# A feed-forward block's opening: one plain chunk in place of two, and two product pairs whose gate blocks are also loaded plain

## Chip, cores and metric
The kernel runs on one core of one Trainium2 chip. The metric is device time in microseconds (us) of one execution. The kernel before takes 2849.59 us (median of three runs, 2848.89 to 2852.01).

## What is computed
A two-layer encoder trunk in fp32 over 768 tokens (512 of one request, 256 of another), model width 1024. Each layer is feed-forward, token mixer, feed-forward:

```python
def swiglu_ffn(x, w1, w2):            # w1: 1024 x 5632, w2: 2816 x 1024
    gate, up = jnp.split(x @ w1, 2, axis=-1)
    return (jax.nn.silu(gate) * up) @ w2

for li in range(2):
    x = x + 0.5 * swiglu_ffn(rmsnorm(x, norm_g[li, 0]), ffn_w1[li, 0], ffn_w2[li, 0])
    x = x + mixer(rmsnorm(x, norm_g[li, 1]))     # layer 0 HGRN2, layer 1 windowed attention
    x = x + 0.5 * swiglu_ffn(rmsnorm(x, norm_g[li, 2]), ffn_w1[li, 1], ffn_w2[li, 1])
```

The change touches only the four feed-forward blocks, called f0 to f3 here in the order in which they run (f0, HGRN2, f1, f2, window attention, f3).

## The kernel before
**Numbers.** Every fp32 factor is split into a rounded part hi and a remainder lo, and a product is three matmuls: hi by hi, hi by lo, lo by hi. ScalarE (ACT) makes hi by a cast, VectorE (DVE) makes lo by a subtraction; for weights these are L166 with L167 (1024 wide) or L199 with L200, for activations both stand in `split` (L266, L267).

**Chunks and products.** The hidden width of 2816 is 22 chunks of 128. A chunk has a gate block and an up block of the weights, each 1024 by 128. Tokens are taken in two halves of 384, the model width in two halves of 512. A chunk is computed in one of two ways:

- *Plain* (`up_plain`): for each token half, 24 matmuls of 128x384 for gate and 24 for up, 96 for the chunk (L261 to L263).
- *Pair* (`up_pair`): gate and up, with the two token halves, make a 2x2 block product that is done by Strassen's seven products (Winograd's form), p1 to p7, of 12 matmuls each, 84 in all (L421). The weight side is combined from four quarter blocks a11, a12 (gate) and a21, a22 (up), the token side from b00, b10, b01, b11 (model half, token half) and four sums t1 to t4. p1 and p2 use b00 and b10 only, and p1 + p2 is just the gate block of the first token half. p7 uses t3, p5 t1, p4 t4, p6 t2, and p3 uses b11.

**Order of a feed-forward block.** `ffn` goes through five groups g of four chunks: up products of the group, then `down_quad`, 126 matmuls of 128x512 (L479), whose results are added to x by DVE (L501). Two chunks are left for the end. In group 0 of every block the first two chunks are plain, and they go first: chunk 0 and chunk 1 on token half 0, then both on token half 1; only then come the pairs of chunks 2 and 3. The reason for plain work in front is in the code's deferred steps: when a block begins, only the first token half has been normalised and transposed. `run_later`, called in the plain chunks' loops, carries out one deferred step at a time between matmuls: the transposes of the second half in two parts (`turn`, L323 and L326, with splits L266 and L267), and `sums`, which makes t1 to t4 by eight subtractions of 128x768 on DVE (L350, L351, L353, L354) and eight splits of 128x768 (ACT L266, DVE L267).

**Weights.** A queue (`plan`, `plan_quad`) lists every weight block in the order of use. `load_next` brings raw blocks into a ring of four raw tiles `wr` (512 KB each, on SP's DMA queue); a pair takes two of them, one for gate and one for up, and for p7 a third small tile `s` (256 KB). GpSimd's queue (POOL) issues accumulating DMAs (`into`, L141): s += a11, and a21 += a22 in place. The remaining combinations are DVE additions in place: a11 += a21 (L206, behind the split for p1) and a12 += a11 (L210, behind the split for p2); they are called the **first add** and the **second add** below. Each split fills a tile of a ring `w` of eight; `held` counts them, and `done` frees one and stages the next steps of the queue as far as eight allow. So a raw tile is free once the last split that reads it has run, and the next load of the queue goes into it. A `down_quad` takes four raw tiles at once, and its first add is 1024 wide.

**Order on the engines.** The program is written in the order of these calls, and a scheduler arranges the instructions of each engine; each engine then carries its own list out strictly in order, waiting on semaphores.

Of the kernel before, what the change touches and what calls it, by code (L numbers as in the profile page):

```python
# [12 lines left out]
AF = mybir.ActivationFunctionType  # L13
# [23 lines left out]
PLAIN = 2  # L37
# [5 lines left out]
UP = ("p1", "p7", "p2", "p5", "p4", "p6", "p3")  # L43
DOWN = ("p1", "p2", "p5", "p4", "p7", "p6", "p3")
# [3 lines left out]
class Trunk:  # L48
# [123 lines left out]
    def quad_steps(self, key, raws, srcs, order):  # L172
# [31 lines left out]
        def p1():  # L204
            split("p1", [a11])
            nc.vector.tensor_add(a11, a11, a21)  # L206

        def p2():
            split("p2", [a12])
            nc.vector.tensor_add(a12, a12, a11)  # L210

        steps = {
            "p1": p1,
            "p2": p2,
            "p3": lambda: split("p3", [a12]),
            "p4": lambda: split("p4", [a22]),
            "p5": lambda: split("p5", [a21], nc.gpsimd if up else None),
            "p6": lambda: split("p6", [a11]),
            "p7": lambda: split("p7", s3),
        }  # L220
        return [(1 if up else 2, steps[name]) for name in order]
# [176 lines left out]
    def up_plain(self, tag, j, half):  # L398
        pss = []
        for c in range(2):  # L400
            wh, wl = self.take((tag, j, c))
            ps = self.ps(H)
            for k in range(NC):
                b = self.operand(f"b{k // 4}{half}", k % 4)
                self.mm3(ps, (wh[:, k, :], wl[:, k, :]), b, k == 0, k == NC - 1)
                if half == 0 and k in (((), (2, 6)), ((3, 7), (3, 7)))[j][c]:
# [9 lines left out]
    def product(self, key, name, src, ps, first, last):  # L416
        wh, wl = self.take((*key, name))
        for k in range(4):
            a, b = (wh[:, k, :], wl[:, k, :]), self.operand(src, k)
# [9 lines left out]
        self.done((*key, name))  # L429

    def up_pair(self, tag, j):
        nc = self.nc
        key = (tag, j)
        a, b, c, d = (self.ps(H) for _ in range(4))
        v, w, t = (self.tmp(H) for _ in range(3))
        p = lambda name, ps, first, last: self.product(key, name, FACTOR[name], ps, first, last)
        p("p1", a, True, False)
        nc.scalar.copy(v, a)
        p("p7", c, True, False)
        nc.scalar.copy(w, c)  # L440
        p("p2", a, False, True)
        nc.scalar.activation(a, a, AF.Silu)
# [60 lines left out]
    def ffn(self, tag, next_row):  # L503
        for g in range(GROUPS):
# [7 lines left out]
            def gather(ts, kp):  # L512
                self.mix(ts[0], ts[1], ts[2], ts[3], lambda name, src: put(name, src, kp))

            if g == 0:
                ts = {}
                for half in range(2):
                    for j in range(PLAIN):
                        t = ts[2 * j + half] = self.up_plain(tag, j, half)
                        name = f"b{j}{half}"  # L520
                        if name != "b01":
                            put(name, t, 0)
                gather(ts, 0)
                self.run_later(len(self.deferred))
            for kp in range(2):
                if g == 0 and kp == 0:
                    continue
                ts = []
                for j in range(2):
                    for half, t in enumerate(self.up_pair(tag, 4 * g + 2 * kp + j)):  # L530
# [751 lines left out]
```

## Time and profile before
| | |
|---|---|
| median of three runs | 2849.59 us |
| profiled execution | 2852.12 us |
| its span | 2850.3 us (1.8 us lie around it) |
| mean granted TensorE clock | 0.998 |
| busy: PE, DVE, ACT, POOL | 98%, 76%, 46%, 12% |
| L421 (pair products) | 6720 matmuls of 128x384 |
| L479 (down products) | 2520 matmuls of 128x512 |

Starts of the stages of group 0, in us from the span's start:

| block | first pair product | first down product |
|---|---|---|
| f0 | 55.31 | 85.17 |
| f1 | 1106.00 | 1135.12 |
| f2 | 1605.54 | 1634.66 |
| f3 | 2382.71 | 2411.83 |

In a timeline row the columns are start, duration, engine, line, operation, output and inputs, form, and count; a bracket at the end gives the idle time ahead and what ended it. Matmuls overlap, so their cost is the distance of their starts and not their duration: the 84 of one pair take 14.57 us (0.1735 each), 18 of a down product 4.28 (about 0.23 each with what follows). The same holds for DVE, whose duration of 0.95 for a 128x768 subtraction goes with starts 0.87 apart, and in the same way 0.60 for 512 wide, 0.47 for 384 wide and 1.13 for 1024 wide.

### The profile page before, as it was taken

Reading aid. Unit: us, or ns where it says so; the run is one execution under the profiler, and the core shown is the slowest. Engines: PE = TensorE matmul, PEld = TensorE weight load, DVE = VectorE, ACT = ScalarE, POOL = GpSimd, SP = SyncE. Lnnn points to the kernel's source line nnn. Section 1 sums busy time; section 2 is a strip of 40 time slices with the busy share of each in tenths; the row PEclk is TensorE's granted clock in tenths of the full one; section 3 lists DMA queues with packets and bytes.
Section 4 is the critical chain, followed back from the end, with each engine's and each line's share of the span. In section 5 each row is a group of like instructions: output and inputs, shape, how many; then the busy total and the mean of one; then the engine's idle time right before and its main releaser. Section 6 shows DMA issues by size and latency. Waiting matters only on the chain. (4 is left out here: it accounts for less than half of the span.)

```text
span 2850.3 us, 40558 instructions
## 1 busy us (share of the span) xinstructions
PE 2796.7 (98%) x15225; PEld 2554.2 (90%) x15225; DVE 2173.2 (76%) x3750; ACT 1318.9 (46%) x2454; POOL 355.1 (12%) x402
## 2 busy tenths in 40 slices
PE   8999999999999999999999999999999899999998
PEld 8899999889899889998998998999888789989997
DVE  7788787468577658878878887887848878788877
ACT  7344443434344336434444643444458755434443
POOL 1111111000000001111111111111002211111110
PEclk9999999999999999999999999999999999999999
DMA  6554454311111133555444355545422113555443
GB/s 165 127 125 122 116 134 121 115 44 39 44 39 38 60 97 86 132 127 122 123 119 114 84 134 127 122 121 124 126 71 75 37 51 90 135 126 125 117 121 96
DMA packets 330101, 291.37 MB, mean 102 GB/s; under 512 B 11608, under 2 KB 257840, under 8 KB 329904
## 3 DMA queue, kind: packets, MB, share of 16 engines
q1 hardware_dynamic: 294064, 212.43, 25.4%
q0 software_dynamic: 31680, 62.93, 12.6%
q10 hardware_dynamic: 4160, 13.42, 1.3%
q8 instruction: 119, 1.95, 0.3%
q14 instruction: 78, 0.64, 0.1%
HBM read 216.39 MB, written 9.44 MB: 79 GB/s over the span
## 5 line engine op out<-in xcount | busy, mean ns | idle before, releaser
L421 PE MATMUL ps<-big,w 128*128 128x384 f32 x6720 | 1172.8, 334 | 3.1 <-DVE tA L444 2.9
L421 PEld LDWEIGHTS ps<-big,w 128*128 128x128 f32 x6720 | 1165.4, 188 | 8.8 <-DVE tA L444 7.2
L199 ACT CAST w<-wr 128x512 fp32r<-128x512 f32 x600 | 416.1, 707 | 722.7 <-PE ps L421 321.0
L479 PE MATMUL ps<-w,big 128*128 128x512 f32 x2520 | 586.8, 391 | 17.4 <-DVE x L501 17.4
L479 PEld LDWEIGHTS ps<-w,big 128*128 128x128 f32 x2520 | 469.4, 188 | 129.7 <-DVE x L501 17.3
L200 DVE TENSOR_TENSOR w<-wr,w 128x512 fp32r<-128x512 f32 (+1 forms) x520 | 438.1, 853 | 95.7 <-ACT w L199 87.0
L501 DVE SCALAR_TENSOR_TENSOR x<-ps,x 128x512 f32<-128x512 f32 x468 | 305.5, 682 | 20.5 <-PE ps L479 10.2
L141 POOL DMA_DIRECT2D s<-wr x120 | 105.4, 878 | 1333.4 <-DMA wr<-in_ffn_w_dram 583.0
L261 PE MATMUL ps<-w,big 128*128 128x512 f32 x624 | 249.8, 400 | 0.2
L263 PE MATMUL ps<-w,big 128*128 128x512 f32 x624 | 245.2, 393 | 2.5 <-DVE big L330 1.3
L262 PE MATMUL ps<-w,big 128*128 128x512 f32 x624 | 244.4, 392 | 0.0
L266 ACT CAST big<-tA 128x384 fp32r<-128x384 f32 x296 | 148.0, 513 | 175.0 <-DVE tA L449 72.0
L261 PE MATMUL ps<-big,w 128*128 128x384 f32 (+2 forms) x640 | 220.8, 346 | 3.3 <-ACT big L266 2.0
L262 PE MATMUL ps<-big,w 128*128 128x384 f32 (+2 forms) x640 | 216.8, 339 | 0.7 <-DVE big L267 0.5
L263 PE MATMUL ps<-big,w 128*128 128x384 f32 (+2 forms) x640 | 215.7, 337 | 0.0
L167 DVE TENSOR_TENSOR w<-wr,w 128x1024 fp32r<-128x1024 f32 x92 | 111.6, 1222 | 83.6 <-ACT w L166 59.7
L141 POOL DMA_DIRECT2D wr<-wr x100 | 87.5, 875 | 680.0 <-DVE tA L350 319.8
L267 DVE TENSOR_TENSOR big<-tA,big 128x384 fp32r<-128x384 f32 x296 | 164.2, 566 | 7.9 <-ACT big L266 4.4
L206 DVE TENSOR_TENSOR wr<-wr,wr 128x512 f32<-128x512 f32 (+1 forms) x100 | 79.3, 793 | 114.5 <-DMA wr<-wr 85.9
L166 ACT CAST w<-wr 128x1024 fp32r<-128x1024 f32 x92 | 96.6, 1052 | 120.5 <-PE ps L262 99.7
L263 PEld LDWEIGHTS ps<-w,big 128*128 128x128 f32 x624 | 117.4, 188 | 28.8 <-DVE big L330 2.0
L261 PEld LDWEIGHTS ps<-w,big 128*128 128x128 f32 x624 | 117.8, 189 | 22.3 <-issue 0.6
(170 smaller groups left out, 3317.2 us busy)
## 6 DMA issues: line engine op xcount, KB each, us to landing
wr<-in_ffn_w_dram SPq DMA_DIRECT2D x264, 512.0 KB, 3.9
s<-in_ffn_w_dram SPq DMA_DIRECT2D x120, 256.0 KB, 3.0
s<-wr POOLq DMA_DIRECT2D x120, 256.0 KB, 4.0
wr<-wr POOLq DMA_DIRECT2D x80, 256.0 KB, 4.0
wr<-in_hg_w_in_dram SPq DMA_DIRECT2D x40, 512.0 KB, 3.8
wr<-wr POOLq DMA_DIRECT2D x20, 512.0 KB, 4.6
spill<-x ACTq DMA_DIRECT2D x12, 512.0 KB, 3.0
x<-spill ACTq DMA_DIRECT2D x12, 512.0 KB, 3.3
```

Source lines behind the costliest of these rows:

```text
L141: self.nc.gpsimd.dma_start(out, src, accum_op=ALU.add)
L167: self.nc.vector.tensor_sub(lo, raw, hi.bitcast(F32))
L199: nc.scalar.copy(h, src)
L200: (eng or nc.vector).tensor_sub(l, src, h.bitcast(F32))
L261: nc.tensor.matmul(out, a[0], b[0], start=first, stop=False)
L262: nc.tensor.matmul(out, a[0], b[1], start=False, stop=False)
L263: nc.tensor.matmul(out, a[1], b[0], start=False, stop=last)
L266: self.nc.scalar.copy(hi, src)
L267: self.nc.vector.tensor_sub(lo, src, hi.bitcast(F32))
L421: self.nc.tensor.matmul(ps, a[x], b[y], start=first and k == 0 and i == 0, stop=k == 3 and i == 2, skip_group_check=True,)
L479: nc.tensor.matmul(ps, a[x], w[y], start=name == chain and kp == 0 and q == 0, stop=kp == 1 and q == 2, skip_group_check=True,)
L501: self.nc.vector.scalar_tensor_tensor(x, ps, c, x, ALU.mult, ALU.add)
```

## The change
Only chunk 0 stays plain. Chunks 1 and 2 become pairs that are *opened*: their gate blocks are loaded and split a second time as plain 1024-wide tiles (key "gate"), and between the two token halves of chunk 0 `open_pairs` multiplies these by b00 (p1 of both) and b10 (p2 of both). That gives the gate of the first token half, and with it p1's value for the rest. After the second token half of chunk 0, the opened pairs compute only p7, p5, p4, p6 and p3 (the order `REST`). In that order the first add stands behind the split for p7 and the second behind that for p4, and the lo split of p5 runs on DVE, where an unopened pair has it on GpSimd. Chunk 3 is a whole pair as before. Deferred steps run at k = 2 and 6 of chunk 0's up block and after each of the four products of `open_pairs`.

```diff
-PLAIN = 2
+PLAIN = 1
+OPENED = range(PLAIN, PLAIN + 2)
+REST = ("p7", "p5", "p4", "p6", "p3")
...
+        own = {"p1": [a11], "p2": [a12], "p3": [a12], "p4": [a22], "p5": [a21], "p6": [a11], "p7": s3}
+        second = lambda: nc.vector.tensor_add(a11, a11, a21)
+        fourth = lambda: nc.vector.tensor_add(a12, a12, a11)
+        after = {"p7": second, "p4": fourth} if order == REST else {"p1": second, "p2": fourth}
+        def step(name):
+            split(name, own[name], nc.gpsimd if order == UP and name == "p5" else None)
+            if name in after:
+                after[name]()
...
             if i < PLAIN:
                 self.plan((tag, i, 0), gate, (NC, P))
                 self.plan((tag, i, 1), up, (NC, P))
+                for j in OPENED:
+                    self.plan((tag, j, "gate"), w1[:, j * P : (j + 1) * P], (NC, P))
             else:
-                self.plan_quad((tag, i), (gate, up), (NC, P), UP)
+                self.plan_quad((tag, i), (gate, up), (NC, P), REST if i in OPENED else UP)
...
+    def open_pairs(self, tag, js):
+        opened = {j: (self.ps(H), self.tmp(H)) for j in js}
+        for part in range(2):
+            for j, (a, v) in opened.items():
+                key = (tag, j, "gate")
+                w = tuple(t[:, 4 * part : 4 * part + 4, :] for t in self.take(key))
+                self.multiply(a, w, FACTOR["p2" if part else "p1"], not part)
+                if part:
+                    self.done(key)
+                    self.nc.scalar.activation(a, a, AF.Silu)
+                else:
+                    self.nc.scalar.copy(v, a)
+                self.run_later()
+        return opened
...
             if g == 0:
-                for half in range(2):
-                    for j in range(PLAIN):
-                        t = ts[2 * j + half] = self.up_plain(tag, j, half)
...
+                plain = [self.up_plain(tag, 0, 0)]
+                put("b00", plain[0], 0)
+                opened = self.open_pairs(tag, OPENED)
                 self.run_later(len(self.deferred))
+                plain.append(self.up_plain(tag, 0, 1))
```

In the changed file the lines move: the first add is L207, the second L208, the weight splits L169 and L202, the activation splits L261 and L262, the subtractions of `sums` L345, L346, L348 and L349, the plain matmuls L256 to L258, the down matmuls L496; the pair products stay L421.

Per feed-forward block the instruction lists differ so: 96 plain matmuls less, 84 pair matmuls more (24 of them in `open_pairs`), so 12 matmuls less; two loads of 512 KB more, one of 256 KB more, two accumulating DMAs more; on DVE one pair's worth of combinations (seven instructions of 128x384) and four weight splits of 512 more, one first and one second add more, two multiplications less; on GpSimd one split less.

Three places show how the lists move; names are the program's own tiles.

**f0, DVE, the weights of the second chunk.** Before: wr_186 and wr_188 are the raw gate and up blocks of chunk 1, x_108 is the last block of tokens, big_274 the transposed second half.

```order
L306 TENSOR_SCALAR big_252<-x_108,stat_253 128x1024
L167 TENSOR_TENSOR w_307<-wr_186,w_306 128x1024
L167 TENSOR_TENSOR w_395<-wr_188,w_394 128x1024
L464 TENSOR_TENSOR x_108<-x_108 128x512
L267 TENSOR_TENSOR big_291<-big_274,big_291 128x2x384
L267 TENSOR_TENSOR big_294<-big_274,big_294 128x2x384
```

After: wr_186 and wr_188 are the plain gate blocks of chunks 1 and 2, wr_194 and wr_196 the raw blocks of the pair of chunk 1.

```order
L301 TENSOR_SCALAR big_252<-x_108,stat_253 128x1024
L207 TENSOR_TENSOR wr_194<-wr_194,wr_196 128x512
L169 TENSOR_TENSOR w_311<-wr_186,w_310 128x1024
L208 TENSOR_TENSOR wr_194<-wr_194 128x512
L481 TENSOR_TENSOR x_108<-x_108 128x512
L262 TENSOR_TENSOR big_291<-big_274,big_291 128x2x384
L262 TENSOR_TENSOR big_294<-big_274,big_294 128x2x384
L262 TENSOR_TENSOR big_303<-tA_300,big_303 128x384
L262 TENSOR_TENSOR big_348<-big_331,big_348 128x2x384
L262 TENSOR_TENSOR big_351<-big_331,big_351 128x2x384
L169 TENSOR_TENSOR w_355<-wr_188,w_354 128x1024
```

Both adds of the pair of chunk 1 now stand around the split of the first gate block, and the split of the second gate block (on ACT its cast too) stands behind the splits of the second token half.

**f1, DVE, the start of `sums`.** big_9086 and big_9125 (before), big_9101 and big_9140 (after) are the transposed second half. Before:

```order
L267 TENSOR_TENSOR big_9103<-big_9086,big_9103 128x2x384
L267 TENSOR_TENSOR big_9106<-big_9086,big_9106 128x2x384
L267 TENSOR_TENSOR big_9142<-big_9125,big_9142 128x2x384
L267 TENSOR_TENSOR big_9145<-big_9125,big_9145 128x2x384
L350 TENSOR_TENSOR big_9125<-big_9086,big_9125 128x768
L413 TENSOR_TENSOR tA_9151<-tA_9151,ps_9072 128x384
L351 TENSOR_TENSOR big_9086<-big_8961,big_9086 128x768
```

After, with wr_9020 and wr_9022 the raw blocks of the pair of chunk 2:

```order
L262 TENSOR_TENSOR big_9118<-big_9101,big_9118 128x2x384
L262 TENSOR_TENSOR big_9121<-big_9101,big_9121 128x2x384
L207 TENSOR_TENSOR wr_9020<-wr_9020,wr_9022 128x512
L208 TENSOR_TENSOR wr_9020<-wr_9020 128x512
L262 TENSOR_TENSOR big_9157<-big_9140,big_9157 128x2x384
L262 TENSOR_TENSOR big_9160<-big_9140,big_9160 128x2x384
L345 TENSOR_TENSOR big_9140<-big_9101,big_9140 128x768
L410 TENSOR_TENSOR tA_9166<-tA_9166,ps_9087 128x384
L346 TENSOR_TENSOR big_9101<-big_8976,big_9101 128x768
```

The two adds of chunk 2's pair are now in front of the splits and of the whole chain of `sums`. On PE the first pair products there are, before, p1, p7 and p2 of chunk 2 (big_8978 and big_9041 are operands of the first token half, big_9180 and big_9196 the two model quarters of t3):

```order
L421 MATMUL ps_9397<-big_8978,w_9270 128x384 x6
L421 MATMUL ps_9397<-big_8981,w_9270 128x384 x6
L421 MATMUL ps_9399<-big_9180,w_9274 128x384 x6
L421 MATMUL ps_9399<-big_9196,w_9274 128x384 x6
L421 MATMUL ps_9397<-big_9041,w_9302 128x384 x6
L421 MATMUL ps_9397<-big_9044,w_9302 128x384 x6
```

and after, p7 of chunk 1 with pieces of p5 (big_9199 and big_9215 are the quarters of t3, big_9191 and big_9207 those of t1):

```order
L421 MATMUL ps_9350<-big_9199,w_9246 128x384 x6
L421 MATMUL ps_9351<-big_9191,w_9250 128x384 x3
L421 MATMUL ps_9350<-big_9215,w_9246 128x384
L421 MATMUL ps_9351<-big_9191,w_9250 128x384 x3
L421 MATMUL ps_9351<-big_9207,w_9250 128x384 x4
L421 MATMUL ps_9350<-big_9215,w_9246 128x384 x5
```

PE's first pair product no longer uses the first half's operands but t3.

**f1, DVE, the end of chunk 3's pair.** Before, wr_9005 and wr_9007 are its raw blocks; the splits of w_9481 and w_9496 are for p6 and p3:

```order
L200 TENSOR_TENSOR w_9465<-wr_9007,w_9465 128x512
L200 TENSOR_TENSOR w_9481<-wr_9005,w_9481 128x512
L447 TENSOR_TENSOR tA_9401<-tA_9401,ps_9398 128x384
L200 TENSOR_TENSOR w_9496<-wr_9005,w_9496 128x512
L448 TENSOR_TENSOR tA_9403<-ps_9399,tA_9401 128x384
```

After, wr_9302 and wr_9304 are its raw blocks, and w_9511 and w_9526 are for p6 and p3:

```order
L202 TENSOR_TENSOR w_9511<-wr_9302,w_9511 128x512
L346 TENSOR_TENSOR tA_9346<-tA_9166,tA_9346 128x384
L348 TENSOR_TENSOR tA_9166<-tA_9166,tA_9352 128x384
L464 TENSOR_TENSOR tA_9175<-tA_9175,ps_9462 128x384
L262 TENSOR_TENSOR big_9448<-tA_9346,big_9448 128x384
L349 TENSOR_TENSOR tA_9353<-tA_9353,tA_9166 128x384
L202 TENSOR_TENSOR w_9526<-wr_9302,w_9526 128x512
```

The hidden chunks' own sums (384 wide), which before ran ahead of these splits, now stand between the splits for p6 and p3 of chunk 3, the last that read its raw tiles.

More of the change, by code (lines that the diff above doesn't have):

```diff
@@ L202, in split @@
             self.staged[(*key, name)] = (view(hi), view(lo), 1 if up else 2)
[L204 to L221, printed above, removed]
+        own = {"p1": [a11], "p2": [a12], "p3": [a12], "p4": [a22], "p5": [a21], "p6": [a11], "p7": s3}
[6 more added lines that the diff above has]
+                after[name]()
+        return [(1 if up else 2, lambda name=name: step(name)) for name in order]
     def stage_next(self):
@@ L428, in product, with up_pair @@
                 )
-        self.done((*key, name))
-    def up_pair(self, tag, j):
+    def open_pairs(self, tag, js):
[12 more added lines that the diff above has]
+        return opened
+    def up_pair(self, tag, j, opened=None):
         nc = self.nc
         key = (tag, j)
[L434 to L438, printed above, removed]
+        a, v = opened or (self.ps(H), self.tmp(H))
+        b, c, d = (self.ps(H) for _ in range(3))
+        w, t = (self.tmp(H) for _ in range(2))
+        p = lambda name, ps, first, last: self.product(key, name, FACTOR[name], ps, first)
+        if not opened:
+            p("p1", a, True, False)
+            nc.scalar.copy(v, a)
         p("p7", c, True, False)
         nc.scalar.copy(w, c)
-        p("p2", a, False, True)
-        nc.scalar.activation(a, a, AF.Silu)
+        if not opened:
+            p("p2", a, False, True)
+            nc.scalar.activation(a, a, AF.Silu)
         p("p5", d, True, False)
```

24 lines of the change are left out of this document (12 added, 12 removed).

## The prediction
> **What bounds the kernel now.** I read the page first, then PE's waits, then the chain of waits, and then timelines at the head of each feed-forward block.
>
> ```profile
> span 2850.3 us, 40558 instructions
> PE 2796.7 (98%) x15225; PEld 2554.2 (90%) x15225; DVE 2173.2 (76%) x3750; ACT 1318.9 (46%) x2454; POOL 355.1 (12%) x402
> L421 PE MATMUL ps<-big,w 128*128 128x384 f32 x6720 | 1172.8, 334 | 3.1 <-DVE tA L444 2.9
> ```
> ```profile
> PE ps L479 <- DVE x L501: 17.4, 37, 0.5
> ```
> ```profile
> 2382.87 14.57 PE ps L421 x84
> ```
>
> TensorE is busy 98% of the span, so work taken from it counts in full as long as the other engines keep feeding it. A matmul of 128x384 costs 14.57/84 = 0.1735 us in a dense stream. PE's largest wait is for DVE in the down products, 37 times at most 0.5 us. So the kernel is bound by PE, with DVE second, and DVE's 76% is a mean over unequal stages:
>
> ```profile
> 1064.00:1106.00 42.00, 41.91 (x254) 40.64 (x252) 37.63 (x51) 31.64 (x56) 3.89 (x3) 1.00 0.20 46
> 1106.00:1135.00 29.00, 29.00 (x169) 29.00 (x169) 21.44 (x34) 14.37 (x25) 3.96 (x4) 1.00 0.46 118
> 1135.00:1165.00 30.00, 29.39 (x129) 23.69 (x128) 29.50 (x48) 10.11 (x18) 4.75 (x5) 1.00 0.56 138
> ```
>
> These are f1's plain stage, its two pairs and its first down products (length, then busy time of PE, weight loads, DVE, ACT, POOL). DVE works 37.6 of 42 us in the first and 29.5 of 30 in the third: beside the plain chunks and in the down products nothing can be added to it, or made late on it, without PE noticing. Only beside the pairs is there slack.
>
> **What goes.** The program's lists have 12 matmuls less per block: 12 x 0.1735 = 2.08 us, four times 8.3 us (0.29%). That is certain, since it is in the instruction lists; the rest is whether PE gets its operands in time.
>
> **Step 1: the t-sums are wanted earlier.** Chunk 0 on its second half takes 48 matmuls where two chunks took 96, so p7, the first product on t3, comes 48 x 0.1735 = 8.33 us before the old end of the plain stage. In f1:
>
> ```profile
> 1106.00 0.68 PE L421 MATMUL ps<-big,w 128*128 128x384 f32 x3
> ...
> 1135.12 4.28 PE L479 MATMUL ps<-w,big 128*128 128x512 f32 x18
> 1139.57 0.70 PE L479 MATMUL ps<-w,big 128*128 128x512 f32 x2 [0.17 <-DVE x L501]
> ```
> ```profile
> 1078.76 1.83 DVE L267 TENSOR_TENSOR big<-big,big 128x768 fp32r<-128x768 f32 x2 [1.52 <-ACT big L266]
> 1082.17 1.83 DVE L267 TENSOR_TENSOR big<-big,big 128x768 fp32r<-128x768 f32 x2 [1.58 <-ACT big L266]
> 1083.91 0.95 DVE L350 TENSOR_TENSOR big<-big,big 128x768 f32<-128x768 f32 x1
> 1084.78 0.55 DVE L413 TENSOR_TENSOR tA<-tA,ps 128x384 f32<-128x384 f32 x1
> ...
> 1119.37 0.69 DVE L200 TENSOR_TENSOR w<-wr,w 128x512 fp32r<-128x512 f32 x1
> 1129.67 1.22 DVE L206 TENSOR_TENSOR wr<-wr,wr 128x1024 f32<-128x1024 f32 x1 [5.21 <-DMA wr<-wr]
> ...
> 1138.74 0.68 DVE L501 SCALAR_TENSOR_TENSOR x<-ps,x 128x512 f32<-128x512 f32 x1
> ```
>
> So p7 starts at 1106.00 - 8.33 = 1097.67. DVE's list in front of it has two new rows, the two adds, between the splits that began at 1078.76 and those at 1082.17. The first add needs a21 += a22, which POOL issues and a DMA carries out:
>
> ```profile
> 1079.67 0.86 POOL L141 DMA_DIRECT2D wr<-wr  x1 [1.92 <-issue]
> ```
> ```profile
> wr<-wr POOLq DMA_DIRECT2D x1, 256.0 KB, 3.3
> ```
>
> It lands at 1079.67 + 3.3 = 1082.97. (I take the landing of the old first pair's for the new second pair's: the tiles stand in the same raw places, behind as many loads.) Then two adds of 512 at 0.60 each, so the splits begin at about 1084.2 and not at 1082.17: DVE would have been idle for 1.58 us there, but the wait for the DMA outlasts it. All of `sums` stands behind this. From 1084.2 to the last subtraction the new list holds eight subtractions and seven splits of 768 at 0.87, two rows of 384 at 0.47 and two weight splits at 0.60, 15.2 us, so to 1099.4; then ACT casts t4's and t3's second quarter, about 0.75 each, and hi of t3 is there at 1100.8. PE wants it after p7's first six and three of p5's matmuls, at 1097.67 + 9 x 0.1735 = 1099.2. **A wait of about 1.6 us** per block. Bounds: none if the accumulation lands by 1080.6, where the two adds fit into DVE's old idle time, and 3 us if two more weight splits or a late cast come in between. f2 and f3 have the same lists, and I give them 1.6 too.
>
> **Step 2: the first down products lose their lead.** Below, the first add of a down quad is L206 of 128x1024; behind it DVE has a fixed chain (about 9 us) up to the first L501, for which PE waits.
>
> ```profile
> 1218.22 1.23 DVE L206 TENSOR_TENSOR wr<-wr,wr 128x1024 f32<-128x1024 f32 x1 [5.55 <-issue]
> ```
> ```profile
> 1223.30 4.28 PE L479 MATMUL ps<-w,big 128*128 128x512 f32 x18
> 1228.12 1.15 PE L479 MATMUL ps<-w,big 128*128 128x512 f32 x4 [0.54 <-DVE x L501]
> ```
> ```profile
> 1628.79 1.23 DVE L206 TENSOR_TENSOR wr<-wr,wr 128x1024 f32<-128x1024 f32 x1 [4.79 <-DMA wr<-wr]
> ...
> 2406.18 1.23 DVE L206 TENSOR_TENSOR wr<-wr,wr 128x1024 f32<-128x1024 f32 x1 [5.01 <-DMA wr<-wr]
> ```
> ```profile
> 1634.66 14.29 PE L479 MATMUL ps<-w,big 128*128 128x512 f32 x62
> ...
> 2411.83 6.54 PE L479 MATMUL ps<-w,big 128*128 128x512 f32 x27
> ```
>
> Lead is the first L479's start less L206's. It is 5.45 in f1 with a gap of 0.17, 5.08 in the later group at 1223 with 0.54, 5.87 in f2 and 5.65 in f3 with none: gap = 5.62 - lead, where positive. Now the lead after. The ring of four raw tiles has two more tenants, so chunk 3's pair waits for chunk 1's last splits (about 1103.8 on DVE by my walk) where it used to wait for a plain block's, and its own a21 += a22 lands a load, an issue on POOL and an accumulation later, by these rows at 1103.8 + 3.9 + 0.9 + 4.0 = 1112.6:
>
> ```profile
> wr<-in_ffn_w_dram SPq DMA_DIRECT2D x264, 512.0 KB, 3.9
> ...
> wr<-wr POOLq DMA_DIRECT2D x80, 256.0 KB, 4.0
> ```
>
> DVE's first add for chunk 3 stands in order behind that. From there to the split for p3 there are 13 rows of 384 and 6 of 512, 9.7 us, which ends at about 1122.3, against 1119.37 + 0.69 = 1120.06 before. That split frees the raw tile for the down loads; the old distance from it to L206 was 1129.67 - 1120.06 = 9.61, so L206 comes at about 1131.9, with a little for ACT 1132.1. PE's first L479 comes at 1135.12 - 2.08 + 1.6 = 1134.6. The lead shrinks from 5.45 to 2.5, by 2.95 us; a split that stood behind the add (1.13) now stands ahead of it, which gives that back. So the gap is 5.62 - 2.5 - 1.13 = **2.0 in f1**, and with the same 2.95 lost, 1.6 in f2 and 1.8 in f3. Bounds: the old gaps, if chunk 3's loads are as early as before, and 2.7, if ACT is late as well.
>
> **Step 3: f0.** There the block starts with nothing staged.
>
> ```profile
> 26.26 0.87 POOL L141 DMA_DIRECT2D wr<-wr  x1 [2.45 <-DMA wr<-in_ffn_w_dram]
> ```
> ```profile
> 28.43 2.35 DVE L167 TENSOR_TENSOR w<-wr,w 128x1024 fp32r<-128x1024 f32 x2
> ```
> ```profile
> 34.61 1.60 ACT L266 CAST big<-big 128x768 fp32r<-128x768 f32 x2
> ```
> ```profile
> 28.21 0.44 PE L261 MATMUL ps<-big,w 128*128 128x384 f32 x1 [1.23 <-ACT w L166]
> ...
> 85.17 4.28 PE L479 MATMUL ps<-w,big 128*128 128x512 f32 x18
> 89.99 2.29 PE L479 MATMUL ps<-w,big 128*128 128x512 f32 x9 [0.54 <-DVE x L501]
> ```
>
> DVE's first add, new ahead of the first gate's lo split, waits for 26.26 + 3.3 = 29.56; the split then begins at 30.1 in place of 28.43, and PE waits about 1.2 to 1.6 for it. The second gate's cast now stands on ACT behind the second half's splits, which end at 34.61 + 1.60 = 36.2; with a copy and its own 1.05 it is there at about 37.6, PE asks for it at about 35.8, and waits 1.7. So 2.9 in all, and I put the first down gap at 0.6 more than the 0.54 shown (as late a lead, less what PE itself is late).
>
> **Sum against the profiled execution (2852.12).** f0: 2.9 + 0.6 - 2.1 = +1.4. f1: 1.6 + 2.0 - 0.2 - 2.1 = +1.3. f2: 1.6 + 1.6 - 2.1 = +1.1. f3: 1.6 + 1.8 - 2.1 = +1.3. Together +5.1.
>
> **The clock.** One stretch of the trace shows a price for new idle time:
>
> ```profile
> 2230.00:2234.50 4.50, 2.46 (x13) 1.53 (x13) 4.50 (x10) 3.26 (x11) 3.89 (x4) 1.00 0.58 166
> 2234.60:2238.00 3.40, 3.40 (x10) 2.54 (x9) 3.12 (x9) 1.30 (x2) 0.00 (x0) 0.51 0.21 78
> ```
> ```profile
> 2232.71 0.33 PE L1144 MATMUL ps<-ident_r,big 128*128 128x128 f32 x1 [1.27 <-POOL big L1138]
> ...
> 2233.95 0.33 PE L1144 MATMUL ps<-ident_r,big 128*128 128x128 f32 x1 [0.68 <-POOL big L1138]
> ...
> 2279.04 0.53 PE L910 MATMUL ps<-ident_r,big 128*128 128x128 f32 x4 [1.87 <-DVE big L267]
> ```
>
> After 1.27 and 0.68 us of idle close together the granted clock was 0.51 for 3.4 us, a loss of 3.4 x 0.49 = 1.7 us; after 1.87 in one piece it was not. The walk has some eight waits of 1 to 2 us, of which I let one cost such a stretch: +1.7, with nought and four (6.8) as the ends. [...]
>
> **The forecast** is +5.1 + 1.7 = +6.8, so 2858.9 against the profiled execution. That execution was 2.5 above the median of the runs shown (2849.59); against the median I forecast 2849.6 + 6.8 = 2856.4, rounded to **2856**.
>
> **Rivals.**
> - *The operands come in time.* Should the accumulation land 2.4 us earlier (by 1080.6) and chunk 3's loads not be held up, both waits go, and the full 8.3 remain: 2841.3; with half a us of waits in each block, 2843. For it: DVE has 1.5 us holes at 1078 and 1082 into which the adds fit, and slack beside the pairs (21.4 of 29). Against it: the measured landing of 1082.97, and the add standing ahead of `sums` in a list that runs strictly in order. Chance 0.18.
> - *The gain is eaten, no more.* Step 1's and f0's waits come (3 x 1.6 + 2.9 = 7.7) and step 2's do not, since DVE, with 7.5 us of slack beside the pairs, catches up: 2849.6 - 8.3 + 7.7 = 2849.0. Or both come at half their size, which gives about the same. Chance 0.27.
> - *Slower through the raw ring alone.* Chunk 3's loads are the mechanism that decides for slower: each us by which its last split is later than PE's own shift costs one us at the first L501, from a lead of 5.62 on. If it is late by 5 and not by 3, 2 us more come in each of four blocks; with a second half clock stretch that gives 2856 + 8 + 1.7 = 2866. Chance 0.12.
> - My forecast, with its own range of 2852 to 2861, has 0.43.
>
> That the change does not do what it says can be excluded, as the lists show the missing matmuls.
>
> **Range and chances.** I leave out times below 2843 and above 2863, some 0.1 each. A difference of 0.2% (5.7 us) is about what a measurement of this kernel can tell from no change: that is below 2843.9 or above 2855.3. Faster: most of the first rival, 0.16. Slower: two thirds of the forecast's case (0.28), all of the third rival (0.12) and a little of the second (0.04), 0.44. Same: 0.40.
>
> **What would show it.** In the changed profile: 48 matmuls fewer on PE; PE's first p7 in f1 about 8 us earlier, with a wait for ACT or DVE (a split of t3) of 1 to 2 us just behind it; L207 ahead of `sums` with idle time that a DMA ended; the first wait for L501's new line grown to about 2 us in each of the four blocks, once each; and the other waits of that kind unchanged. If L207 shows no wait for a DMA, or L496's first wait stays at 0.5, steps 1 or 2 are wrong, and the time is that of a rival.

## The result and the profile after

The changed kernel takes **2879.23 us** (median, 2875.94 to 2883.70, five runs) where the kernel before takes 2850.39 (median of five): a ratio of 1.0105, interval 1.0093 to 1.0116, so about 29 us slower. The forecast of 2856 had the sign right, but the loss is about four and a half times the 6.4 us that were forecast, and the time lies well above the range of 2843 to 2863.

The profiled execution has a span of 2876.9 us, 26.6 more than before, and a mean granted clock of 0.994 where it was 0.998. From the page of the changed kernel, section 1 and the group of pair products (the third part of a group's row is the idle time of PE just ahead of it and what ended it):

```profile
PE 2802.6 (97%) x15177; PEld 2554.5 (89%) x15177; DVE 2191.5 (76%) x3794; ACT 1328.7 (46%) x2474; POOL 352.2 (12%) x406
...
L421 PE MATMUL ps<-big,w 128*128 128x384 f32 x7056 | 1244.4, 336 | 21.0 <-ACT tA L456 8.0
```

The 48 matmuls are gone (15225 before, 15177 now), yet PE's time ahead of pair products grew from 3.1 to 21.0 us. PE's waits of the changed kernel by what ended them (total, times, longest):

```profile
PE ps L496 <- DVE x L518: 16.2, 34, 0.6
PE ps L421 <- ACT tA L456: 8.0, 4, 2.8
...
PE ps L421 <- ACT big L261: 5.9, 3, 2.4
PE ps L256 <- ACT big L261: 3.8, 4, 2.0
PE ps L421 <- ACT w L168: 3.2, 2, 1.9
...
PE ps L318 <- DVE big L301: 3.0, 4, 1.3
...
PE ps L257 <- DVE big L262: 2.0, 4, 0.7
PE ps L421 <- DVE tA L461: 1.9, 5, 0.8
...
PE ps L421 <- DVE w L169: 1.1, 1, 1.1
```

The first row, the down products, did not grow: 16.2 us against 17.4 before. Nearly all that is new stands ahead of the first down product of each block. Those starts, by PE's timeline of the changed kernel:

```profile
1147.87 4.28 PE L496 MATMUL ps<-w,big 128*128 128x512 f32 x18
```
```profile
1653.29 4.28 PE L496 MATMUL ps<-w,big 128*128 128x512 f32 x18
```
```profile
2439.32 4.28 PE L496 MATMUL ps<-w,big 128*128 128x512 f32 x18
```

Against 1135.12, 1634.66 and 2411.83 before, PE is 12.8, 18.6 and 27.5 us late at f1, f2 and f3.

**The clock.** In the profiled execution of the changed kernel the granted clock falls to half for 3.4 us eight times (and once more at the very end), in that of the kernel before twice (and once more at the end): six stretches more, at 1.7 us each about 10 us. The mean clocks, which are rounded, say the same within their rounding: (1 - 0.994) x 2876.9 = 17 us of lost full speed against (1 - 0.998) x 2850.3 = 6. The other executions of the changed kernel have mean clocks of 0.994 to 0.996 and take about as long; at 0.996 the term is only some 6 us. Two of the stretches stand in f3; the windows give length, busy time of PE, weight loads, DVE, ACT and POOL, then the clock:

```profile
2400.60:2404.00 3.40, 3.40 (x13) 3.40 (x12) 3.40 (x6) 1.20 (x3) 0.35 (x1) 0.52 0.49 141
...
2417.40:2420.80 3.40, 3.40 (x14) 3.40 (x13) 3.28 (x6) 1.63 (x4) 0.60 (x1) 0.56 0.26 44
```
```profile
2400.08 5.16 PE L421 MATMUL ps<-big,w 128*128 128x384 f32 x19 [2.40 <-ACT big L261]
```
```profile
2416.82 6.37 PE L421 MATMUL ps<-big,w 128*128 128x384 f32 x26 [1.76 <-ACT tA L456]
```

Both begin within about 1 us of the end of one of the new waits. Three others of the six stand at new waits too (at 38.7 and 69.4 us in f0 and at 1615.7 in f2); the sixth follows on a wait in the HGRN2 layer that was there before (last section). So the sum of the profiled executions is: -8.3 for the matmuls, about +21 for the waits (29 us in the rows of the feed-forward blocks other than the down products, where the kernel before has 7; the down products themselves wait 1 less), about +10 for the clock; that makes 23 of 26.6. Where the remaining 3 to 4 us go these rows do not show.

**Where the waits come from in f1.** DVE, ACT and PE around the opened pairs:

```profile
1092.33 0.69 DVE L207 TENSOR_TENSOR wr<-wr,wr 128x512 f32<-128x512 f32 x1 [2.42 <-issue]
...
1123.34 0.69 DVE L207 TENSOR_TENSOR wr<-wr,wr 128x512 f32<-128x512 f32 x1 [1.78 <-DMA wr<-wr]
1123.95 0.55 DVE L466 TENSOR_TENSOR tA<-tA,ps 128x384 f32<-128x384 f32 x1
```
```profile
1119.75 0.62 ACT L201 CAST w<-s 128x512 fp32r<-128x512 f32 x1 [2.41 <-DMA s<-wr]
...
1124.53 0.51 ACT L261 CAST big<-tA 128x384 fp32r<-128x384 f32 x1 [3.64 <-DVE tA L466]
...
1125.47 0.47 ACT L456 COPY tA<-ps 128x384 f32<-128x384 f32 x1
```
```profile
1110.57 13.52 PE L421 MATMUL ps<-big,w 128*128 128x384 f32 x75 [1.65 <-ACT big L261]
1126.00 10.70 PE L421 MATMUL ps<-big,w 128*128 128x384 f32 x60 [1.91 <-ACT tA L456]
```

Read the last pair first. PE waits 1.65 us for t3 (the sums, late), and 15 us later 1.91 us ahead of the second opened pair's p4, which adds onto p7's bank and must wait until ACT has copied that bank (L456). ACT was free for 3.64 us before, but the row ahead of the copy in its list waits for DVE's L466, and DVE's L466 stands behind chunk 3's first add (L207), which waits for the DMA a21 += a22 of chunk 3. One late transfer passes through the lists of three engines: 1.78 us idle on DVE ahead of L207, 3.64 on ACT ahead of L261, 1.91 on PE ahead of p4.

### The profile page after: what moved, and what is told of

It reads as the page before. It is cut to its first block, busy times and chain, and to the rows that moved or that the text cites. A ratio compares the mean times of both kernels' runs of the same rounds, so it can differ in the third digit from the quotient of the medians.

```text
span 2876.9 us, 40598 instructions
## 1 busy us (share of the span) xinstructions
PE 2802.6 (97%) x15177; PEld 2554.5 (89%) x15177; DVE 2191.5 (76%) x3794; ACT 1328.7 (46%) x2474; POOL 352.2 (12%) x406
## 5 line engine op out<-in xcount | busy, mean ns | idle before, releaser
L421 PE MATMUL ps<-big,w 128*128 128x384 f32 x7056 | 1244.4, 336 | 21.0 <-ACT tA L456 8.0
L421 PEld LDWEIGHTS ps<-big,w 128*128 128x128 f32 x7056 | 1230.8, 189 | 32.0 <-ACT tA L456 9.7
L201 ACT CAST w<-wr 128x512 fp32r<-128x512 f32 (+1 forms) x608 | 421.4, 705 | 706.3 <-PE ps L421 309.0
L496 PE MATMUL ps<-w,big 128*128 128x512 f32 x2520 | 586.4, 391 | 16.5 <-DVE x L518 16.2
L496 PEld LDWEIGHTS ps<-w,big 128*128 128x128 f32 x2520 | 469.7, 188 | 128.1 <-DVE x L518 16.3
L202 DVE TENSOR_TENSOR w<-wr,w 128x512 fp32r<-128x512 f32 (+1 forms) x532 | 440.9, 839 | 96.5 <-ACT w L201 88.1
L256 PE MATMUL ps<-w,big 128*128 128x512 f32 x624 | 249.9, 400 | 0.2
L258 PE MATMUL ps<-w,big 128*128 128x512 f32 x624 | 245.1, 393 | 2.5 <-DVE big L325 1.3
L257 PE MATMUL ps<-w,big 128*128 128x512 f32 x624 | 244.5, 392 | 0.0
L261 ACT CAST big<-tA 128x384 fp32r<-128x384 f32 x296 | 147.9, 513 | 193.8 <-DVE tA L466 83.0
L256 PE MATMUL ps<-big,w 128*128 128x256 f32 (+2 forms) x512 | 177.9, 349 | 3.9 <-ACT big L261 3.8
L207 DVE TENSOR_TENSOR wr<-wr,wr 128x512 f32<-128x512 f32 (+1 forms) x104 | 82.2, 790 | 125.8 <-DMA wr<-wr 96.7
L257 PE MATMUL ps<-big,w 128*128 128x256 f32 (+2 forms) x512 | 174.2, 340 | 2.0 <-DVE big L262 2.0
L169 DVE TENSOR_TENSOR w<-wr,w 128x1024 fp32r<-128x1024 f32 x92 | 111.9, 1222 | 83.9 <-ACT w L168 78.3
L258 PE MATMUL ps<-big,w 128*128 128x256 f32 (+2 forms) x512 | 173.0, 338 | 0.0
L262 DVE TENSOR_TENSOR big<-tA,big 128x384 fp32r<-128x384 f32 x296 | 164.9, 568 | 6.5 <-ACT big L261 4.0
L168 ACT CAST w<-wr 128x1024 fp32r<-128x1024 f32 x92 | 96.7, 1052 | 121.8 <-PE ps L257 100.9
L258 PEld LDWEIGHTS ps<-w,big 128*128 128x128 f32 x624 | 117.4, 188 | 28.8 <-DVE big L325 2.0
L256 PEld LDWEIGHTS ps<-w,big 128*128 128x128 f32 x624 | 117.8, 189 | 22.3 <-issue 0.6
```

The lines of the kernel that those rows point to most:

```text
L169: self.nc.vector.tensor_sub(lo, raw, hi.bitcast(F32))
L201: nc.scalar.copy(h, src)
L202: (eng or nc.vector).tensor_sub(l, src, h.bitcast(F32))
L256: nc.tensor.matmul(out, a[0], b[0], start=first, stop=False)
L257: nc.tensor.matmul(out, a[0], b[1], start=False, stop=False)
L258: nc.tensor.matmul(out, a[1], b[0], start=False, stop=last)
```

## The experiments

All ratios are to the kernel before, run beside the kernel on the same chip; that kernel's median was 2850.34 beside the first four, 2852.82 beside the next three, 2853.02 beside three more and 2852.43 beside the last two. "Wait" is PE's idle time ahead of pair products in the group's row of each profile; it and the clock are those of the one execution that was profiled.

| run | median us | ratio (interval) | wait us | clock |
|---|---|---|---|---|
| before | 2850.39 | | 3.1 | 0.998 |
| changed | 2879.23 | 1.0105 (1.0093 to 1.0116) | 21.0 | 0.994 |
| 1 adds of the opened pairs pinned | 2870.34 | 1.0072 (1.0055 to 1.0089) | 22.3 | 0.993 |
| 2 adds of chunks 1 to 3 pinned | 2870.24 | 1.0067 (1.0051 to 1.0083) | 21.8 | 0.996 |
| 3 chunk 3's adds late | 2876.79 | 1.0091 (1.0075 to 1.0107) | 18.3 | 0.996 |
| 4 two plain chunks, opened late | 2868.00 | 1.0063 (1.0045 to 1.0081) | 14.4 | 0.996 |
| 5 run 2, copy first | 2864.03 | 1.0039 (1.0026 to 1.0052) | 19.8 | 0.995 |
| 6 own blocks | 2862.50 | 1.0040 (1.0026 to 1.0054) | 11.7 | 0.997 |
| 7 runs 5 and 6 together | 2866.73 | 1.0049 (1.0034 to 1.0064) | 17.5 | 0.995 |
| 8 own blocks, chunk 3's adds late | 2854.58 | 1.0003 (0.9993 to 1.0013) | 9.8 | 0.999 |
| 9 own blocks, chunk 3's adds pinned | 2857.06 | 1.0015 (1.0006 to 1.0025) | 8.4 | 0.998 |
| 10 run 9, copy first | 2853.22 | 1.0004 (0.9994 to 1.0013) | 8.9 | 0.997 |
| 11 run 8 with f0 as before | 2849.38 | 0.9988 (0.9979 to 0.9997) | 2.7 | 0.997 |
| 12 run 10 with f0 as before | 2851.13 | 0.9994 (0.9985 to 1.0003) | 6.4 | 0.999 |

**Theories after the result.** A: a first add that waits for its DMA holds DVE's strict order up. B: DVE has too much to do, whatever its order. C: chunk 3's raw blocks come late, and whichever instruction waits for them carries that on. D: the two extra gate blocks are the cause, as loads and as tenants of the raw ring.

**Run 1.** The opened pairs' adds are queued on DVE behind their p4 split:

```diff
+        pinned = order == REST
+        after = {} if pinned else ...
         def step(name):
             split(name, own[name], ...)
+            if pinned and name == "p4":
+                with self.tc.issue_after(self.behind):   # the lo split of p4
+                    second()
+                    fourth()
```

> The changed kernel, with both adds of the opened pairs (chunks 1 and 2) queued on DVE behind the pair's own split for p4, so that they no longer stand in front of the block's head and of the sums. Theory A (a first add that waits for its accumulating DMA holds DVE's strict order up, and PE behind it): the waits at the heads of f0, f2 and f3 and most of the wait at the first p7 go, 5 to 8 us and one to three half clock stretches of 1.7 us: 2866 to 2872. Theory B (DVE simply has too much work there, its order does not matter): within 3 us of the changed kernel, 2876 to 2882. The waits ahead of the second opened pair's p4 (8.0 us in four) stay in both.

2870.34, as A expects, and the rows that A names go: the row for the cast of t3 (5.9 us) is missing, and of the 8.8 us at the heads of the blocks 4.8 are left, all of them in f0. But the waits ahead of p4 did not stay, as was expected: that for the copy grew from 8.0 to 13.7 us, that for a subtraction of DVE's (L461 in the changed kernel) from 1.9 to 6.5:

```profile
PE ps L428 <- ACT tA L463: 13.7, 5, 4.6
PE ps L428 <- DVE tA L468: 6.5, 6, 3.8
```

B falls, by the median; A is part of it, and most of what it gains is given back one stage later. The profile is of the slowest of the run's four executions (2876.95, clock 0.993): its gain in idle time is only about 2 us, so the 9 us of the median are a result of the times, which this trace does not take apart.

**Run 2.** The same with `pinned = up and key[1] in (1, 2, 3)`.

> As the run before, with chunk 3's adds queued behind its p4 split too. Theory A: the waits of PE for the copy of p7's bank ahead of the second opened pair's p4 (2.8, 1.9, 1.5 and 1.8 us) go as well, with a stretch or two of half clock: 2853 to 2863. Theory C (chunk 3's raw blocks come late because the ring of four has more tenants, and the copy on ACT is behind casts that wait for these blocks, whatever DVE does): no better than the run before, 2864 to 2872. Theory B: 2876 to 2882.

2870.24: no better than run 1, as C says and not A. With DVE no longer in the chain, ACT waits for chunk 3's transfer itself, with the cast for its p5, again ahead of the copy:

```profile
1121.62 0.62 ACT L201 CAST w<-wr 128x512 fp32r<-128x512 f32 x1 [4.53 <-DMA wr<-wr]
1122.14 0.47 ACT L463 COPY tA<-ps 128x384 f32<-128x384 f32 x1
```
```profile
1122.67 22.64 PE L428 MATMUL ps<-big,w 128*128 128x384 f32 x120 [3.51 <-ACT tA L463]
```

**Run 3.** Only the place in the code: for chunks 1 to 3 the first add right ahead of p6, the second right ahead of p3.

```diff
...
+        ahead = {"p6": second, "p3": fourth} if up and key[1] in (1, 2, 3) else {}
         def step(name):
+            if name in ahead:
+                ahead[name]()
             split(name, own[name], ...)
```

> The changed kernel with only the order in the code changed for chunks 1 to 3: the first add right ahead of the p6 split, the second right ahead of the p3 split. On DVE's list the opened pairs' adds stay where they were (at the head), chunk 3's first add moves four to six rows back, behind the recombination of the first opened pair. Theory A: the waits ahead of the second opened pair's p4 (8.0 us) go or shrink below 2, the others stay: 2866 to 2873. Theory C: unchanged, 2876 to 2882.

2876.79, between the two expectations. The wait for the copy halved (8.0 to 4.3 us), so chunk 3's add is a link of the chain; most other waits stayed, those for DVE's subtraction (1.9 to 3.6 us) and in the down products (16.2 to 18.2) grew, and the time hardly moved.

**Run 4.** Two plain chunks as before the change, `open_pairs` only after all plain work; the gate blocks of chunks 2 and 3 are loaded in addition.

```diff
-PLAIN = 1
+PLAIN = 2
...
-                for j in OPENED:
+                for j in OPENED if i == PLAIN - 1 else ():
                     self.plan((tag, j, "gate"), ...)
...
+                # plain chunks 0 and 1 on half 0, then on half 1, as before the change
                 self.run_later(len(self.deferred))
+                opened = self.open_pairs(tag, OPENED)
```

> Two plain chunks as before (no matmul is saved), and the next two pairs opened with plain gate blocks of their own, but only after all plain work, so that the two extra loads of 512 KB, the extra splits and the extra tenants of the raw ring are there, while the first p7 comes 48 matmuls later than before the change and not 48 earlier. Theory A (what costs is that things are wanted earlier than the order on DVE delivers them): 2848 to 2856. Theory D (the additional loads and splits cost by themselves): 2862 or more.

2868.00. This is the run that turned the explanation round: p7 comes later than in the kernel before, no matmul is saved, and 18 us are lost all the same, the largest part of the new waits again ahead of p4:

```profile
PE ps L421 <- ACT tA L456: 6.9, 3, 3.5
```

So the loss comes with no product wanted earlier than before, as D has it and not A. By itself the run does not tell the gate blocks from the rest of the opened form (order `REST`, p5's lo split on DVE), which it also has; run 6 does.

**Run 5.** Run 2, and in the opened pairs the copy of p7's bank is issued ahead of the casts that its release stages:

```diff
-        p("p7", c, True, False)
-        nc.scalar.copy(w, c)
+        self.multiply(c, self.take((*key, "p7")), FACTOR["p7"], True)
+        copied = nc.scalar.copy(w, c).ins
+        with self.tc.issue_after(copied) if opened else nullcontext():
+            self.done((*key, "p7"))
```

> The second run (adds of chunks 1 to 3 pinned), and in the opened pairs the copy of p7's bank is issued on ACT ahead of the casts that its own release stages, so that chunk 3's cast for p5, which waited 4.5 us for its accumulating DMA, no longer stands in front of the copy that PE's p4 waits for. Theory C' (chunk 3's raw blocks land late, and ACT's strict order carries that to PE by the copy): the 12.8 us of waits for the copy fall below 3, with one to three half clock stretches less: 2853 to 2860. Theory C'' (the data of chunk 3 are late for PE itself): the same wait returns at chunk 3's own products, 2866 to 2872.

2864.03, between the two. The wait for the copy fell from 12.8 to 3.7 us, but that at the products which need a subtraction of DVE's grew from 5.8 to 12.5, in f1 at the same pair's p3. ACT's cast for chunk 3 began at 1121.16 after 3.78 us of idle time (1121.62 after 4.53 in run 2), and DVE's list comes to the subtraction (L470) only behind it:

```profile
PE ps L428 <- DVE tA L470: 12.5, 9, 3.2
```
```profile
1121.16 0.62 ACT L201 CAST w<-wr 128x512 fp32r<-128x512 f32 x1 [3.78 <-issue]
```
```profile
1125.75 19.75 PE L428 MATMUL ps<-big,w 128*128 128x384 f32 x96 [3.10 <-DVE tA L470]
```

In all of runs 1, 2 and 5 the wait ahead of the pair products moves on and hardly shrinks (22.3, 21.8 and 19.8 us, against 21.0). The transfer is late, and pinning one engine's list hands most of the delay to the next; run 5 still gains 0.28 points on run 2.

**Run 6.** The changed kernel without the gate loads: an opened pair's p1 and p2 are split from its own raw blocks, first of all its steps.

```diff
+OPEN = ("p1", "p2") + REST
...
-                for j in OPENED:
-                    self.plan((tag, j, "gate"), ...)
+            # in load_next: p1 and p2 of both opened pairs are staged ahead of the rest of either
+            if how == OPEN:
+                at = next((i for i, e in enumerate(self.loaded) if len(e) > 2), len(self.loaded))
+                self.loaded.insert(at, (0, steps[:2]))
+                self.loaded.append((2, steps[2:], "rest"))
+                return
```

> The changed kernel without the two extra gate loads of 512 KB and their two 1024 wide splits: p1 and p2 of the opened pairs are split from the pair's own raw blocks, as in an unopened pair, right at the start. Matmuls, adds and their places in the code as in the changed kernel. Theory D (extra loads and tenants of the raw ring cost): 2855 to 2868. Theory A (the order of DVE's adds alone): within 4 us of the changed kernel.

2862.50, in the middle of what D expects: of the 1.05% lost, 0.65 points go with the gate blocks. The splits of the two kernels are as many elements, so what goes is the loads and their place in the ring. The second opened pair's a21 += a22 in f1 shows why. It is issued here, and there in the changed kernel:

```profile
1062.11 0.88 POOL L144 DMA_DIRECT2D wr<-wr  x1 [2.03 <-DVE stat L306]
```
```profile
1088.98 0.88 POOL L143 DMA_DIRECT2D wr<-wr  x1 [2.08 <-DMA wr<-in_ffn_w_dram]
```

And here is p7, in the same order:

```profile
1101.48 15.15 PE L425 MATMUL ps<-big,w 128*128 128x384 f32 x84
```
```profile
1107.20 1.73 PE L421 MATMUL ps<-big,w 128*128 128x384 f32 x9
```

Without the gate blocks in the ring the pair takes chunk 0's raw tiles, and its accumulation is issued 39 us ahead of p7 and not 18, so 21 us earlier. What is left ahead of the copy (5.8 us) is chunk 3's add, which waits for its DMA as in the changed kernel:

```profile
1113.71 0.69 DVE L213 TENSOR_TENSOR wr<-wr,wr 128x512 f32<-128x512 f32 x1 [2.73 <-DMA wr<-wr]
```
```profile
1118.45 22.64 PE L425 MATMUL ps<-big,w 128*128 128x384 f32 x120 [1.81 <-ACT tA L458]
```

**Run 7.** The edits of runs 2, 5 and 6 together.

> Both edits of these runs together: own blocks, pinned adds, the copy ahead of the casts. If C' and D are both right, the waits at the heads and at the copy are gone and the 48 matmuls saved remain: 2841 to 2850. If chunk 3's late raw blocks still reach PE: 2852 to 2862.

2866.73, worse than run 6 alone and than both expectations. With own blocks the opened pairs' adds are no longer late, and holding them back behind p4 only delays p6 and p3, which read them, and so the release of the raw tiles that chunk 3 waits for: in f1 chunk 3's a21 += a22 is issued 12.5 us behind p7 (1116.19 and 1103.73), in run 6 it is 6.1 (1107.59 and 1101.48). A pin that helped in run 1 hurts here.

**Runs 8, 9 and 10.** Own blocks; chunk 3's adds alone late in the code (run 8), pinned behind its p4 split (run 9), and pinned with the copy first (run 10).

```diff
+        late = up and key[1] == 3
+        after = {} if late else ...
+        ahead = {"p6": second, "p3": fourth} if late else {}
```

> Own blocks (the sixth run), and chunk 3's first add written ahead of its p6 split, so that it stands seven rows further back on DVE, behind the recombination of the first opened pair. In the sixth run it waited 2.7 us for its accumulating DMA in f1, and DVE's subtraction, ACT's cast and the copy behind it held PE's p4 up (1.1, 1.8, 2.6 and 1.4 us in the four blocks). Theory C (this chain is what is left): those waits go, with up to two half clock stretches: 2850 to 2857. Rival (the wait returns through ACT, whose cast for chunk 3's p5 needs the same DMA): 2859 to 2865.

> The same with chunk 3's adds queued behind its p4 split, six rows further back still. Theory C: as the run before, 2850 to 2857. If instead chunk 3's late adds now delay the release of its raw tiles and so the first down products: the waits ahead of the first L501-like addition grow above 1 us in group 0, 2857 to 2862.

> The same, and the copy of p7's bank ahead of the casts that its release stages. If the cast for chunk 3's p5 is what is left in front of the copy: 3 us or more below the run before, 2846 to 2853; if not, within 2 us of it.

2854.58, 2857.06 and 2853.22: as theory C has it for run 8, at the edge of both expectations for run 9, and for run 10 3.8 us under run 9, at the weak end of the first expectation. Runs 8 and 10 are level with the kernel before, run 9 is 0.15% above it. In run 8's f1 chunk 3's first add goes without waiting, and the whole way from p7 to the first down product is one row, with no wait shown:

```profile
1116.95 0.68 DVE L213 TENSOR_TENSOR wr<-wr,wr 128x512 f32<-128x512 f32 x1
```

```profile
1103.72 35.91 PE L429 MATMUL ps<-big,w 128*128 128x384 f32 x204
1139.47 5.77 PE L502 MATMUL ps<-w,big 128*128 128x512 f32 x23
```

204 matmuls in 1139.47 - 1103.72 = 35.75 us are 0.175 us each, almost the dense 0.1735. And its mean clock is 0.999: with the waits, the half clock stretches are gone too, but for one at 15.5 us, which the kernel before has as well. The 8.3 us of matmuls that it saves come back elsewhere: its pair products still wait 9.8 us where the kernel before has 3.1.

**Runs 11 and 12.** Runs 8 and 10 with f0 as it was before the change (two plain chunks, no opened pair), so 36 matmuls saved.

```diff
+FIRST = {"f0": 2}
+OPENED = {"f0": ()}
...
+                if tag in FIRST:
+                    # plain chunks 0 and 1, as before the change
+                else:
+                    # chunk 0 with the opened pairs
```

> The eighth run (own blocks, chunk 3's first add late) in f1, f2 and f3, and f0 as it was before the change (two plain chunks, no opened pair). In the eighth run's profile f0's first down product came 4.6 us later than before the change, while the way from each block's last group to the next block's first down product was 0.9, 0.1 and 0.7 us shorter than before. So if f0's start, where nothing is staged yet, is what is left: about 4.6 us under the eighth run, 1 to 4 us under the kernel before (2848 to 2852 where that has 2853). If f0's loss is given back later in other places: level with the eighth run, 2853 to 2856.

> The tenth run's structure in f1, f2 and f3, and f0 as before the change. By the same reasoning (f0's first down product 4.3 us late there): 2847 to 2851 where the kernel before has 2853; if f0's loss is given back later: 2852 to 2855.

2849.38 beside 2852.43: ratio 0.9988 with an interval that ends at 0.9997, the one version that beats both kernels, by 3 us of the 6.2 that its 36 matmuls are worth (and as one of twelve whose interval only just leaves 1 out, so not a strong result). Run 12, 2851.13 and 0.9994, is a touch above what f0 alone would give and cannot be told from the kernel before. With f0 as before, run 11's pair products wait 2.7 us and not 9.8 as in run 8, so f0, where nothing is staged when the block begins, held most of what was still lost there.

## Why the prediction was wrong

- *What bounds the kernel; the matmuls saved.* Right: 48 fewer on PE, and in run 8's f1 they come out at 0.175 us.
- *Step 1, the sums are wanted earlier.* Right in mechanism and place, and near in size: 1.6 us were forecast in f1, f2 and f3 each, and the row for L261 shows 1.65, 1.85 and 2.40. That the first add, which waits for its transfer, made it, and not p7's earlier place alone, shows in run 1: with that add out of the way and p7 no later, the row is missing.
- *Step 2, the raw ring.* The cause was right (chunk 3's pair waits for chunk 1's last splits, and its transfers land late), the place was wrong, and this is the step that failed. I followed the delay along DVE only, to the first down products, and gave 2.0, 1.6, 1.8 and 0.6 us there. The runs show it some 25 us earlier: it holds ACT's copy, which PE needs for the second opened pair's p4, 8.0 us in four waits (1.9 in f1). The down products' waits stayed at 0.6 or less each, which the prediction had named as the sign that step 2 is wrong. That the 8.0 us come near the 6.0 forecast for another place is luck. I had also put the landing of chunk 3's transfer at 1112.6, or 1120.5 once shifted by the 7.9 us that f1 begins later (its first transposes at 1071.99 and 1064.06); the add went at 1123.34.
- *The rest of the ring.* I took the second opened pair's raw blocks to stand "in the same raw places, behind as many loads" as the old first pair's. That is wrong, they stand two loads further back and in the gate blocks' places; yet the time taken from it was nearly right: the accumulation was issued at 1088.98, 1081.1 without the shift, where 1079.67 was assumed. What was missed is the other side: without the gate blocks (run 6) it is issued 21 us earlier against p7, and 0.65 of the 1.05 points go. The forecast asked what is wanted earlier and gave the two extra loads no price of their own.
- *Put at nothing: the heads of f1, f2 and f3.* There too chunk 1's first add was moved on DVE ahead of the block's norm, in f2 even ahead of the last additions to x of the block before. It waited 2.22, 3.56 and 3.46 us, with the norm and so PE's first transposes and products behind it. In f2:

```profile
1571.04 0.69 DVE L207 TENSOR_TENSOR wr<-wr,wr 128x512 f32<-128x512 f32 x1 [3.56 <-issue]
1571.65 0.68 DVE L518 SCALAR_TENSOR_TENSOR x<-ps,x 128x512 f32<-128x512 f32 x1
```
```profile
1576.36 0.88 PE L318 MATMUL ps<-ident_r,big 128*128 128x128 f32 x6 [0.99 <-DVE big L301]
```

  The rows L318, L256 and L257 together are 8.8 us, against 3.0 in those rows before; in run 1, where that add stands further back, the waits at these three heads are gone. The list of f0's head showed the same add in the same place; I priced it in f0 and did not look at the other blocks.
- *Step 3, f0.* 2.9 us forecast; 1.06 for L169 and 1.94 for L168 measured there. The price of f0's raw ring came on top (2.83 ahead of p4).
- *The clock.* One stretch of 1.7 us was let in, six more than before came. That is the largest single term that was mis-sized: 1.7 against about 10 in the profiled execution. Four were allowed for, as the far end.

By terms, in the profiled execution: step 1 1 us over the forecast, f0's two waits as forecast; step 2 2 over (8 for 6) and in another place; heads 6 over; clock 8.5 over. That is about 17.5 of the 20 us between the forecast and the measured time. So step 2 had the path wrong, and the number failed above all on two terms, the heads that were put at nothing and the clock. A rival had named the ring as the mechanism that decides for slower, with 2866, and it too reckoned the loss at the down products.

**What stays open.** Whether the gate blocks cost as tenants of the ring or also as traffic was not taken apart; a longer ring was not run. That the half clock stretches follow from the waits rests on their places and on run 8, where both went together; no run filled the waits with other work. Some 3 us of the profiled difference stand in no term.

## What to carry to other kernels

Before an extra block is put into a ring of buffers, follow who gets which slot afterwards, two tenants on: here the accumulation of the pair behind came 21 us closer to its use. In f1 one instruction that waited for a DMA (DVE's L207, 1.78 us) delayed what stood behind it on its engine and, through that, ACT's copy and PE's p4 (1.91 us), so a late transfer must be followed through every list that waits on it, not along one engine; pinning one list handed most of the wait to the next (runs 1, 2 and 5), and what ended it was an earlier transfer together with a later place for the add (run 8), where the later place alone (run 3) or the earlier transfer alone (run 6) did not. Short waits of PE can be dearer than their length, here by 1.7 us where a stretch of 3.4 us at half clock followed, as after the waits of 2.40 and 1.76 us in f3.

## What the runs showed of the hardware

The clock fell to half for about 3.4 us after single waits of 1.76 and 2.40 us (above), but not after the 1.91 us in f1, nor after the 1.87 us in the kernel before that the prediction shows. The same wait of 1.74 us in the HGRN2 layer had no such stretch in the kernel before and had one in the changed kernel, with the same instructions:

```profile
587.16 1.09 PE L671 MATMUL ps<-big,big 128*128 128x128 f32 x5 [1.74 <-ACT big L696]
```
```profile
587.20:590.60 3.40, 3.40 (x25) 3.40 (x26) 2.78 (x5) 0.92 (x1) 0.00 (x0) 1.00 0.00 0
```
```profile
593.69 1.60 PE L687 MATMUL ps<-big,big 128*128 128x128 f32 x8 [1.74 <-ACT big L712]
```
```profile
594.50:597.90 3.40, 3.40 (x19) 3.40 (x18) 2.18 (x4) 0.93 (x1) 0.00 (x0) 0.59 0.00 0
```

So in these two profiles the length of a wait alone does not tell whether a stretch at half clock follows; what else decides was not shown.
